# Operand order of small matmuls in three recurrences, and two stretches instead of five for A's score levels

## The chip, the cores and the metric

The kernel runs on one core of one Trainium2 chip. The metric is the device time of one execution in microseconds; a kernel's time is the median over its runs. TensorE (PE) does the matmuls, VectorE (DVE) and ScalarE (ACT) the elementwise work, GpSimd (POOL) small copies and masks, SyncE (SP) issues most DMAs.

## What is computed

One layer with three recurrent mixers over 16 learned tokens and 256 tokens of width 2048: a gated linear recurrence (A), an mLSTM (B) and RWKV-7 (C), each 1024 wide. All start from one projection of the normalised input and end in three gated branch products, one output product and a norm.

```python
xn = rmsnorm(h, norm_g[l])
(a_q, a_f, a_i, a_z, b_q, ..., c_z, g_a, g_b, g_c) = split_cols(xn @ w_in[l])
y_a, y_b, y_c = hgrn2_mixer(...), mlstm_mixer(...), rwkv7_mixer(...)
merged = (sigmoid(g_a) * (y_a @ w_br[l, 0]) + sigmoid(g_b) * (y_b @ w_br[l, 1])
          + sigmoid(g_c) * (y_c @ w_br[l, 2]))
h = h + merged @ w_out[l]
# A, in one chunk: scores with a decay between positions t and s, channel by channel
att = einsum('bhtd,bhsd,bhtsd->bhts', q, k, pair_decay(cg, cg, causal_mask(length)))
# C, in one chunk: a unit lower triangular solve, then outputs and the next state
u = triangular_solve(eye(length) - l_ab, rhs)
y = einsum(r * exp(cw), s_mat) + r_b @ u + r_k @ v
s_mat = exp(cw[-1]) * s_mat + (b * tail).T @ u + (k * tail).T @ v
```

## The kernel before

**Gemms.** Weights stream in as f32 tiles `raw` (SP queue). ACT casts each to `wh`, DVE subtracts to get the remainder `wl`; the activations are split in the same way (`xH`, `xL`). Each product is three fp32r matmuls, and all of them are named `gp<-...` in the trace after their PSUM tile. Blocks run in a fixed list: the projections of the groups of B, C and A, then for each of the branches B, C, A four pairs of a gate product and a branch product, then the output product. These gemms fill TensorE from 16 us to the end.

**Scans.** The recurrences are Python generators that put their small instructions between the gemm matmuls: `b_scan` (4 heads), `c_scan` (4 groups, PSUM tile `cbank`) and `a_scan` (4 groups, PSUM tile `bank`). A planner (`Order`) advances a generator as the gemm's planned clock moves on, and the framework's scheduler then places every instruction of every engine in one static program, by its own estimate of when its operands are written. TensorE runs its program in order. So where a scan's matmuls are not all estimated ready at the same time, the scheduler puts gemm matmuls between them.

**The places that the change touches.** A *stretch* here is a run of scan matmuls with no gemm matmul between them. All matmuls of the scans except those on `bonesR`, `onesR` with split operands, `wups` and `sel`, and the transposes, are plain f32, and the trace has two records for each of them.

- `colsum` sums a split operand over partitions: first with its high half `h` (written by ACT), then with its low half `l` (written later, by DVE).
- `c_scan`, after its solve: products with `VT` and then `ZT` build the inverse's off-diagonal block, over `p` = 0, 1. `VT` comes by two DMAs, `p` = 0 first. Two copies write `ZT`, `X` and `UV` for the two halves `p`: DVE that of `p` = 0, ACT that of `p` = 1 (`ZT`: ACT both). In each of five chunks: `UV,SC`, `cX,Vm`, then the state product `UV,BT` (four matmuls, `p` = 0 then 1, chunks 0 to 3), then the output products `SC,UV` and `RA,Zs`.
- `a_scan` builds the scores of a 32 by 32 block in five levels, pair by pair: level 4 from `Kb`, `Qb`, levels 0 to 3 from tiles `W` of half width 16, 8, 4 and 2. Each level has two DVE subtractions (`aE`), an exponential on ACT, two DVE products (`aW`), and then `small(li, ...)`, 16 or 18 matmuls of 32 columns. The score levels go to two PSUM banks `pss` and are masked and summed after the last level. `aE`, `aW`, `aKb`, `aQb`, `aC`, `aLF` share a pool of six buffers (tag `wx`).

The first product of branch B (tile `yHB`, the cast of B's result) needs room that the pool of C frees only after its fourth scan; on TensorE it follows the first gate block (`gp<-wh,xH 128x512` and its like).

Of the kernel before, what the change touches and what calls it, by code (L numbers as in the profile page):

```python
# [150 lines left out]
def kernel(  # L151
# [33 lines left out]
    def mm(o, lhsT, rhs, start, stop):  # L185
        nc.tensor.matmul(o, lhsT, rhs, start=start, stop=stop)  # L186
        n = 1
        for d in rhs.shape[1:]:
            n *= d
        od.cost("pe", max(n, 256) / 2400 + 0.003 if lhsT.dtype == F32R else max(4 * n / 2400, 0.04 if lhsT.shape[1] <= 32 else 0.1))  # L190
# [23 lines left out]
    def cbank():  # L214
        return cps.tile([P, 512], F32, name="cbank", tag="s")

    def wc(shape, name, dt=F32):
        return ev.tile(shape, dt, name=name, tag="wc", bufs=6)

    def wx(shape, name, dt=F32):  # L220
        return ev.tile(shape, dt, name=name, tag="wx", bufs=6)
# [8 lines left out]
            yield  # L230

    def colsum(o, w, h, l):
        mm(o, w, h, start=True, stop=False)
        mm(o, w, l, start=False, stop=True)

    def low(l, x, h):
        V.tensor_tensor(out=l, in0=x, in1=h.bitcast(F32), op=ALU.subtract)
# [269 lines left out]
    def c_scan(g, st):  # L507
# [32 lines left out]
        for j in range(2):  # L540
            ps = cbank()
            colsum(ps[:, 0:T], bonesR, HL[:, 0, j, :], HL[:, 1, j, :])
            V.tensor_scalar(out=SQ[:, j, :], in0=ps[:, 0:T], scalar1=1e-24, scalar2=None, op0=ALU.max)
# [26 lines left out]
        for cc in (0, 2, 4):  # L570
# [3 lines left out]
            w = P if n == 2 else 2 * NMETA  # L574
# [46 lines left out]
        for j in range(2):  # L621
            colsum(ps[:, j * SEQ:(j + 1) * SEQ], bonesR, RH[:, j, :], RL[:, j, :])
# [73 lines left out]
        ps = cbank()  # L696
        psz = ps.rearrange("s (q k) -> s q k", k=32)
        ZT = wc([P, 8, 32], "ZT")
        for c in range(4):
            for p in range(2):  # L700
                for j in range(2):
                    r = 64 * p + 32
                    q = 64 * (1 - p)
                    mm(psz[r:r + 32, 4 * j + c, :], SC[q:q + 32, j, c, 0, p, 32:64], VT[q:q + 32, 5 * j + c, :],
                       start=True, stop=True)
        for p in range(2):
            r = 64 * p + 32
            S.copy(out=ZT[r:r + 32], in_=psz[r:r + 32, 0:8, :])
        yield "pe"
        ps = cbank()  # L710
        psz = ps.rearrange("s (q k) -> s q k", k=32)
        for c in range(4):
            for p in range(2):
                for j in range(2):
                    r = 64 * p + 32
                    mm(psz[64 * p:64 * p + 32, 4 * j + c, :], ZT[r:r + 32, 4 * j + c, :], Vm[r:r + 32, j, c, p, 32:64],
                       start=True, stop=True)
# [13 lines left out]
        for c in range(5):  # L731
            nq = 64 if c < 4 else NMETA

            ps = cbank()
            psv = ps.rearrange("s (j p v) -> s j p v", j=4, p=2)
            for j in range(2):
                mm(psv[:, j], SC[:, j, c, 0].rearrange("s p t -> s (p t)"), UV[:, c, j].rearrange("s p v -> s (p v)"), start=True, stop=True)
            X = cp.tile([P, 2, 64], F32, name="cX", tag="cX")
            for p in range(2):
                hs = slice(64 * p, 64 * p + 64)  # L740
                (S.copy if p else V.tensor_copy)(out=X[hs], in_=psv[hs, 0:2, p, :])
            yield "pe"
            ps = cbank()
            psv = ps.rearrange("s (j v) -> s j v", v=64)
            for j in range(2):
                mm(psv[:, j, :], Vm[:, j, c].rearrange("s p t -> s (p t)"), X[:, j, :], start=True, stop=True)
            for p in range(2):
                (S.copy if p else V.tensor_copy)(out=UV[64 * (1 - p):64 * (1 - p) + 64, c, :, p, :],
                                                 in_=psv[64 * p:64 * p + 64, 0:2, :])
            yield "pe"  # L750
            if c < 4:
                ps = cbank()
                psv = ps.rearrange("s (j v) -> s j v", v=64)
                for j in range(2):
                    for p in range(2):
                        hs = slice(64 * p, 64 * p + 64)
                        mm(psv[hs, j, :], BT[:, j, c, hs], UV[:, c, j, p, :], start=True, stop=True)
                Sn = cp.tile([P, 2, 64], F32, name="cS", tag="cS", bufs=2)
                el = E1[:, :, 64 * c + 63:64 * c + 64].broadcast_to([P, 2, 64])
                if St is None:  # L760
                    V.tensor_tensor(out=Sn, in0=psv[:, 0:2, :], in1=el, op=ALU.mult)
                else:
                    V.tensor_tensor(out=Sn, in0=psv[:, 0:2, :], in1=St, op=ALU.add)
                    V.tensor_tensor(out=Sn, in0=Sn, in1=el, op=ALU.mult)
                for p in range(2):
                    (S.copy if p else V.tensor_copy)(out=UV[64 - 64 * p:128 - 64 * p, c + 1, :, p, :],
                                                     in_=Sn[64 * p:64 * p + 64])
            after = od.ready
            ps = cbank()
            psv = ps.rearrange("s (j v) -> s j v", v=64)  # L770
            for j in range(2):
                for p in range(2):
                    mm(psv[64 * p:64 * p + 64, j, 0:nq], UV[:, c, j, p, :], SC[:, j, c, 1, p, 0:nq], start=True, stop=St is None)
                if St is not None:
                    for p in range(2):
                        mm(psv[64 * p:64 * p + 64, j, 0:nq], cst["Zs"][:, p, j, :], RA[:, 1, j, 64 * c:64 * c + nq], start=False, stop=True)
            S.copy(out=Yt[:, :, 64 * c:64 * c + nq], in_=psv[:, 0:2, 0:nq])
            if c < 4:

                for p in range(2):  # L780
                    nc.gpsimd.tensor_copy(out=cst["Zs"][64 * p:64 * p + 64, p], in_=Sn[64 * p:64 * p + 64])
                St = Sn
                od.ready = max(after, od.ready - 0.5)
            yield "pe"
# [11 lines left out]
        for j in range(2):  # L796
            colsum(ps[:, j * SEQ:(j + 1) * SEQ], bonesR, SH[:, j, :], SL[:, j, :])
# [340 lines left out]
    def a_scan(g, st):  # L1138
# [20 lines left out]
        def small(li, lk, lq):  # L1159
            for j in range(2):  # L1160
                pv = pss[j][:, 0:320].rearrange("s (b l t) -> s b l t", b=2, l=5)
                for b in range(8):
                    r = 32 * (b % 4)
                    mm(pv[r:r + 32, 1 - b // 4, li, :], lk[:, j, 32 * b:32 * b + 32], lq[:, j, 32 * b:32 * b + 32],
                       start=True, stop=True)
                if li:
                    o = 320 + 16 * (li - 1)
                    mm(pss[j][96:128, o:o + 16], lk[:, j, T - 32:T], lq[:, j, SEQ:T], start=True, stop=True)


        Kb = wx([P, 2, T], "aKb")
        Qb = wx([P, 2, T], "aQb")
# [3 lines left out]
        S.activation(out=f2(Kb)[:, :, 1], in_=f2(LF)[:, :, 1], func=AF.Exp, scale=-1.0)  # L1176
        V.tensor_tensor(out=f2(Qb)[:, :, 1], in0=f2(Q)[:, :, 1], in1=f2(G)[:, :, 1], op=ALU.mult)
        V.tensor_tensor(out=f2(Kb)[:, :, 1], in0=f2(Kb)[:, :, 1], in1=f2(K)[:, :, 1], op=ALU.mult)
        yield "pe"
        small(4, Kb, Qb)  # L1180

        for li, hf in enumerate((16, 8, 4, 2)):
            W = wx([P, 2, T], f"aW{hf}")
            E = wx([P, 2, T], "aE")
            if hf == 16:
                view = lambda a: a[:, :, 0:SEQ].rearrange("p j (b e) -> p j b e", e=32)
                nb = [P, 2, 8, 16]
            else:
                view = lambda a: a.rearrange("p j (b e) -> p (j b) e", e=2 * hf)
                nb = [P, 2 * T // (2 * hf), hf]  # L1190
            Cv, Ev, Wv, Kv, Qv = (view(a) for a in (C, E, W, K, Q))
            ref = Cv[..., hf - 1:hf].broadcast_to(nb)
            od.ready = od.clk["pe"]
            V.tensor_tensor(out=Ev[..., 0:hf], in0=ref, in1=Cv[..., 0:hf], op=ALU.subtract)
            V.tensor_tensor(out=Ev[..., hf:], in0=Cv[..., hf:], in1=ref, op=ALU.subtract)
            full = (lambda a: a[:, :, 0:SEQ]) if hf == 16 else (lambda a: a)
            S.activation(out=full(E), in_=full(E), func=AF.Exp)
            yield
            V.tensor_tensor(out=Wv[..., 0:hf], in0=Ev[..., 0:hf], in1=Kv[..., 0:hf], op=ALU.mult)
            V.tensor_tensor(out=Wv[..., hf:], in0=Ev[..., hf:], in1=Qv[..., hf:], op=ALU.mult)  # L1200
            yield "pe"
            small(li, W, W)
            yield

        M2 = wx([P, 2, 2, 32], "aM2")
# [99 lines left out]
        for j in range(2):  # L1305
            o = po[:, j * SEQ:(j + 1) * SEQ]
# [204 lines left out]
    for u in range(KT // UK):  # L1511
        h, l = ws.next()
        unit(h, l, u, KT, gw[0][:, 0:T], xH, xL, 0, T, slice(0, P))
        h, l = ws.next()
# [100 lines left out]
    for n, (c0, m) in enumerate(outs):  # L1615
        ps = [gps.tile([P, 512], F32, name="gp", tag="g") for _ in range(2)]
        us = KT * m // 1024
        if n < len(outs) - 1:
            for u in range(us):
                h, l = ws.next()  # L1620
# [55 lines left out]
```

## Time and profile before

| | us |
|---|---|
| runs (3), median | 1255.44 (1253.87 to 1256.13) |
| the profiled execution, its own time | 1253.23 |
| its span, first to last instruction | 1251.5 |
| PE busy | 1228.9 (98%) |
| PE weight load busy | 1114.4 (89%) |
| DVE busy | 875.4 (70%) |
| ACT busy | 661.2 (53%) |

The chain that ended last lies 89% on PE, 6% on DVE, 2% on ACT. Records of matmuls overlap, and their ends are modelled, so the busy time of PE says only that it was hardly ever empty; how fast it works is read from the distance between the starts of neighbouring records. 9226 records stand for 8212 matmuls. The mean granted clock is 0.994.

### The profile page before, as it was taken

To read this page: it belongs to the slowest core of one execution; us is meant where nothing else is said; L and a number is where in the kernel's file an instruction comes from. 1 tells how busy PE (TensorE), PEld (TensorE's weight loads), DVE (VectorE), ACT (ScalarE), POOL (GpSimd) and SP (SyncE) were. 2 spreads that over 40 slices of the span, in tenths; PEclk is the share of its full clock that TensorE was granted. 3 is DMA by queue.
4 is the path that set the end of the run, shared out by engine and by line. 5 is a ranking of instruction groups with operands and counts; after the bars stand their busy time and mean duration, and the time that the engine had idled before them with its cause. 6 is when DMAs were issued, how large, how long until landed. Compare 5 with 4: busy or idle time off the path is not lost.

```text
span 1251.5 us, 23069 instructions
## 1 busy us (share of the span) xinstructions
PE 1228.9 (98%) x9226; PEld 1114.4 (89%) x9226; DVE 875.4 (70%) x1485; ACT 661.2 (53%) x1028; POOL 51.3 (4%) x167
## 2 busy tenths in 40 slices
PE   8999999999999999999999999999999999999997
PEld 8999999999998999989999987888888888888887
DVE  6688996698975889976789985644555565555554
ACT  6765445664445764656665655544444444444444
POOL 3100000000050000000000000000000000000000
PEclk8999999999999999999999999999999999999999
DMA  8646564465563554444554453566766666665563
GB/s 227 189 140 172 153 177 127 119 172 160 152 168 87 169 167 137 144 137 122 161 162 138 128 174 107 187 197 187 223 196 187 191 213 201 190 194 171 186 199 120
DMA packets 173125, 207.43 MB, mean 166 GB/s; under 512 B 22396, under 2 KB 127225, under 8 KB 172633
## 3 DMA queue, kind: packets, MB, share of 16 engines
q1 hardware_dynamic: 172104, 202.73, 55.3%
q0 software_dynamic: 880, 3.22, 0.7%
q8 instruction: 72, 1.18, 0.4%
q14 instruction: 37, 0.30, 0.1%
q10 hardware_dynamic: 32, 0.01, 0.0%
HBM read 202.19 MB, written 3.74 MB: 165 GB/s over the span
## 4 chain that ended last, share of the span: by engine, by line
PE 89%; DVE 6%; ACT 2%; issue 1%; DMA 1%; SPq 0%; ACTq 0%; DVEq 0%
PE gp L186 79%; PE cbank L186 5%; PE bank L186 3%; DVE wl L127 2%; ACT wh L127 1%; PE cbank L193 1%; DMA xt<-in_x_dram 1%; PE bank L193 1%; DVE aM L127 0%; DVE LV L127 0%; DVE BK L127 0%; DVE aY L127 0%; DVE Ltmp L127 0%; DVE UV L127 0%; DVE SC L127 0%
## 5 line engine op out<-in xcount | busy, mean ns | idle before, releaser
L127 DVE TENSOR_TENSOR wl<-raw,wh 128x1024 fp32r<-128x1024 f32 (+1 forms) x370 | 449.0, 1215 | 250.1 <-ACT wh L127 247.9
L127 ACT CAST wh<-raw 128x1024 fp32r<-128x1024 f32 (+1 forms) x370 | 386.3, 1045 | 398.3 <-PE gp L186 369.6
L186 PE MATMUL gp<-xH,wh 128*128 128x272 f32 (+3 forms) x1552 | 450.3, 290 | 0.5 <-DVE cK L127 0.3
L186 PE MATMUL gp<-xH,wl 128*128 128x272 f32 (+3 forms) x1552 | 444.8, 287 | 3.6 <-DVE wl L127 3.6
L186 PE MATMUL gp<-xL,wh 128*128 128x272 f32 (+3 forms) x1552 | 445.4, 287 | 0.0
L186 PEld LDWEIGHTS gp<-xH,wl 128*128 128x128 f32 x1552 | 293.0, 189 | 4.9 <-DVE wl L127 4.2
L186 PEld LDWEIGHTS gp<-xH,wh 128*128 128x128 f32 x1552 | 293.3, 189 | 3.2 <-DVE cK L127 0.5
L186 PEld LDWEIGHTS gp<-xL,wh 128*128 128x128 f32 x1552 | 293.1, 189 | 1.1 <-DVE xL L127 0.2
L186 PE MATMUL gp<-wh,xH 128*128 128x512 f32 x384 | 152.6, 397 | 0.0
L186 PE MATMUL gp<-wh,xL 128*128 128x512 f32 x384 | 152.0, 396 | 0.0
L186 PE MATMUL gp<-wl,xH 128*128 128x512 f32 x384 | 150.9, 393 | 0.0
L186 PEld LDWEIGHTS gp<-wh,xL 128*128 128x128 f32 x384 | 72.1, 188 | 17.5
L186 PEld LDWEIGHTS gp<-wl,xH 128*128 128x128 f32 x384 | 72.3, 188 | 16.0
L186 PEld LDWEIGHTS gp<-wh,xH 128*128 128x128 f32 x384 | 72.2, 188 | 15.8
L186 PE MATMUL gp<-wh,mH 128*128 128x512 f32 (+1 forms) x144 | 51.1, 355 | 0.0
L186 PE MATMUL gp<-wl,mH 128*128 128x512 f32 (+1 forms) x144 | 51.0, 354 | 0.0
L186 PE MATMUL gp<-wh,mL 128*128 128x512 f32 (+1 forms) x144 | 50.9, 354 | 0.0
L127 DVE TENSOR_TENSOR Ltmp<-LU,LV 40x31 f32<-40x31 f32 (+15 forms) x124 | 41.0, 331 | 2.5 <-DMA LU<-scr 0.3
L127 DVE TENSOR_TENSOR LV<-LV,Ltmp 40x31 f32<-40x31 f32 (+15 forms) x124 | 41.0, 331 | 2.4
L186 PEld LDWEIGHTS gp<-wh,mL 128*128 128x128 f32 x144 | 27.2, 189 | 3.8
L186 PEld LDWEIGHTS gp<-wh,mH 128*128 128x128 f32 x144 | 27.2, 189 | 3.8
L186 PEld LDWEIGHTS gp<-wl,mH 128*128 128x128 f32 x144 | 27.2, 189 | 3.6
(410 smaller groups left out, 1488.5 us busy)
## 6 DMA issues: line engine op xcount, KB each, us to landing
raw<-in_w_in_dram SPq DMA_DIRECT2D x288, 512.0 KB, 3.6
raw<-in_w_br_dram SPq DMA_DIRECT2D x48, 512.0 KB, 4.2
raw<-in_w_out_dram SPq DMA_DIRECT2D x32, 512.0 KB, 3.5
hres<-in_x_dram POOLq DMA_DIRECT2D x2, 1024.0 KB, 6.6
raw<-in_w_in_dram SPq DMA_DIRECT2D x4, 256.0 KB
fg<-in_final_norm_g_dram POOLq DMA_DIRECT2D x1, 1024.0 KB, 4.5
out_dram<-hres SPq DMA_DIRECT2D x4, 256.0 KB, 2.3
xt<-in_x_dram SPq DMA_DIRECT2D x3, 320.0 KB, 4.9
```

The lines of the kernel that those rows point to most:

```text
L127: r = f(*a, **k)
L186: nc.tensor.matmul(o, lhsT, rhs, start=start, stop=stop)
L193: nc.tensor.transpose(o, a, i)
```

## The change

Three things. `colsum` multiplies the low half first. In `c_scan` five loops over `p` go over 1, 0 instead of 0, 1, so that the first matmul of each group reads the half that is written last. In `a_scan` the first level is not multiplied at once: levels are collected, and after half widths 8 and 2 the collected ones are multiplied, the newest first. The order of additions within the sums is not touched, apart from `colsum`.

```diff
     def colsum(o, w, h, l):
-        mm(o, w, h, start=True, stop=False)
-        mm(o, w, l, start=False, stop=True)
+        mm(o, w, l, start=True, stop=False)
+        mm(o, w, h, start=False, stop=True)
...
         for c in range(4):
-            for p in range(2):
+            for p in (1, 0):
...
                 for j in range(2):
-                    for p in range(2):
+                    for p in (1, 0):
                         hs = slice(64 * p, 64 * p + 64)
                         mm(psv[hs, j, :], BT[:, j, c, hs], UV[:, c, j, p, :], start=True, stop=True)
...
             for j in range(2):
-                for p in range(2):
+                for p in (1, 0):
                     mm(psv[64 * p:64 * p + 64, j, 0:nq], UV[:, c, j, p, :], SC[:, j, c, 1, p, 0:nq], start=True, stop=St is None)
                 if St is not None:
-                    for p in range(2):
+                    for p in (1, 0):
...
-        yield "pe"
-        small(4, Kb, Qb)
+        todo = [(4, Kb, Qb)]
...
-            yield "pe"
-            small(li, W, W)
+            todo.append((li, W, W))
+
+            if hf in (8, 2):
+                yield "pe"
+                while todo:
+                    small(*todo.pop())
             yield
```

Built, both programs have 8212 matmuls. Those of the scans stand in 200 stretches before and in 170 after: `UV,BT` heads 30 and then 16, `SC,UV` 8 and 4, products with `VT` 6 and 3, with `ZT` 6 and 3, `cX,Vm` 19 and 20, stretches with A's levels 17 and 8, transposes 37 and 39; the rest is equal in number.

PE, first group of C, second chunk from the end of its state products (`UV,BT`, the state product; `gp`, a gemm). Before:

```order
L186 MATMUL gp<-xH,wl 128x272
L186 MATMUL cbank<-UV,BT 64x64
L186 MATMUL gp<-xH,wh 128x272
L186 MATMUL cbank<-UV,BT 64x64 x3
L186 MATMUL cbank<-SC,UV 64x64 x2
L186 MATMUL cbank<-RA,Zs 64x64 x2
```

After, the corresponding chunk:

```order
L186 MATMUL gp<-xL,wh 128x272
L186 MATMUL gp<-xH,wl 128x272
L186 MATMUL gp<-xH,wh 128x272
L186 MATMUL cbank<-UV,BT 64x64 x4
L186 MATMUL cbank<-SC,UV 64x64 x2
L186 MATMUL cbank<-RA,Zs 64x64 x2
```

The one matmul that stood alone has joined the other three; this holds at 14 of the 16 state products (two were whole before).

PE, first group of A, the score levels (`aW_5985`: half width 8; `aW_5873`: 16; `aQb,aKb`: level 4; before, 16 is `aW_5978`). Before, the level of half width 16 alone, between gemm matmuls:

```order
L186 MATMUL gp<-xH,wh 128x256
L186 MATMUL gp<-xL,wh 128x256
L186 MATMUL gp<-xH,wl 128x256
L186 MATMUL bank<-aW_5978 32x32 x16
L186 MATMUL gp<-xH,wh 128x256
```

After:

```order
L186 MATMUL gp<-xH,wl 128x256
L186 MATMUL bank<-aW_5985 32x32 x8
L186 MATMUL bank<-aW_5985 32x16
L186 MATMUL bank<-aW_5985 32x32 x8
L186 MATMUL bank<-aW_5985 32x16
L186 MATMUL bank<-aW_5873 32x32 x16
L186 MATMUL bank<-aQb,aKb 32x32 x8
L186 MATMUL bank<-aQb,aKb 32x16
```

Three levels follow each other; the other two (half widths 2 and 4) stand in a second stretch. In the second and the fourth group C's `VT` or `ZT` products stand inside A's second stretch.

ACT, around the first cast of B's result (`yHB`), where the fourth scan of C ends (`cY`: its output copy; `cSq`, `cSH`: squares for its norm; `ATT`: scores of A's fourth group). Before:

```order
L127 COPY cY<-cbank 128x2x16
L127 COPY ATT<-bank 32x2x64
L127 ACTIVATE cSq_9721<-cY 128x512
L127 ACTIVATE cSH<-cY 128x512
L127 COPY ATT<-bank 32x2x32
L127 COPY ATT<-bank 128x144
L127 COPY ATT<-bank 128x16
L127 ACTIVATE sg<-gp 128x512 x2
L127 ACTIVATE cSq_9721<-cbank,epsc 128x512
L127 CAST yHB<-yB 128x512
```

After:

```order
L127 COPY UV<-cbank 64x2x64
L127 COPY cY<-cbank 128x2x16
L127 CAST yHB<-yB 128x512
L127 ACTIVATE cSq_9728<-cY 128x512
L127 ACTIVATE cSH<-cY 128x512
```

The cast has moved ahead of the squares, the score copies and the gate's `sg`. On PE the last output product of C (`SC,UV`, `RA,Zs` of the fifth chunk) stood one gemm matmul ahead of the first product with `yHB`; now 21 gemm matmuls stand between them. C's fourth scan as a whole stands some 20 gemm matmuls earlier: its `VT` products follow gemm matmul 4742 before and 4722 after.

## Rows read from the trace of the kernel before

**Rows 1.** The page, busy time of each engine, its share and its instructions.

```profile
PE 1228.9 (98%) x9226; PEld 1114.4 (89%) x9226; DVE 875.4 (70%) x1485; ACT 661.2 (53%) x1028; POOL 51.3 (4%) x167
```

**Rows 2.** Waits of PE: who waited for whom, us in total, times, longest.

```profile
PE gp L186 <- DVE wl L127: 3.6, 3, 1.5
PE gp L186 <- ACT yHB L127: 1.3, 1, 1.3
```

**Rows 3.** Timeline of PE, a split state product: start, us, engine, what, records.

```profile
216.10 0.29 PE L186 MATMUL gp<-xL,wh 128*128 128x272 f32 x1
216.23 0.29 PE L186 MATMUL gp<-xH,wl 128*128 128x272 f32 x1
216.45 0.33 PE L186 MATMUL cbank<-UV,BT 128*64 128x64 f32 x2
216.71 0.39 PE L186 MATMUL gp<-xH,wh 128*128 128x272 f32 x1
217.03 0.39 PE L186 MATMUL cbank<-UV,BT 128*64 128x64 f32 x5
...
218.10 0.29 PE L186 MATMUL gp<-xH,wl 128*128 128x272 f32 x1
```

**Rows 4.** Timeline of PE, a state product in one piece, last group.

```profile
755.47 0.39 PE L186 MATMUL gp<-wh,xH 128*128 128x512 f32 x1
755.70 0.40 PE L186 MATMUL gp<-wl,xH 128*128 128x512 f32 x1
756.03 0.49 PE L186 MATMUL cbank<-UV,BT 128*64 128x64 f32 x8
...
757.25 0.40 PE L186 MATMUL gp<-wh,xH 128*128 128x512 f32 x1
```

**Rows 5.** Timeline of PE, two stretches of A: 36 and 108 records.

```profile
469.23 0.29 PE L186 MATMUL gp<-xH,wl 128*128 128x272 f32 x1
469.44 0.57 PE L186 MATMUL bank<-aQb,aKb 128*32 128x32 f32 x36
...
470.18 0.30 PE L186 MATMUL gp<-xL,wh 128*128 128x272 f32 x1
...
484.47 0.28 PE L186 MATMUL gp<-xH,wl 128*128 128x256 f32 x1
484.68 1.33 PE L186 MATMUL bank<-aW 128*32 128x32 f32 x108
...
486.17 0.29 PE L186 MATMUL gp<-xL,wh 128*128 128x272 f32 x1
```

**Rows 6.** Timeline of PE, where C's fourth scan ends.

```profile
767.70 0.50 PE L186 MATMUL gp<-wh,xL 128*128 128x512 f32 x1
...
769.48 0.38 PE L186 MATMUL cbank<-cSH,bonesR 128*128 128x256 f32 x1 [0.85 <-ACT cSH L127]
...
772.15 0.80 PE L186 MATMUL gp<-wh,yHB 128*128 128x512 f32 x1 [1.28 <-ACT yHB L127]
772.74 0.63 PE L186 MATMUL gp<-wl,yHB 128*128 128x512 f32 x1
773.17 0.63 PE L186 MATMUL gp<-wh,yHB 128*128 128x512 f32 x1
```

**Rows 7.** Windows: us, busy PE, PEld, DVE, ACT, POOL, PE clock, DMA.

```profile
450.00:530.00 80.00, 78.17 (x811) 76.12 (x810) 74.83 (x170) 47.56 (x80) 0.32 (x2) 1.00 0.51 144
640.00:730.00 90.00, 86.52 (x962) 83.46 (x961) 81.78 (x185) 50.85 (x84) 0.13 (x1) 1.00 0.53 149
772.00:775.00 3.00, 2.85 (x7) 2.27 (x8) 2.43 (x4) 3.00 (x7) 0.00 (x0) 0.50 0.02 5
```

**Rows 8.** Timeline of DVE and ACT, the two copies ahead of that state product.

```profile
755.38 0.28 DVE L127 COPY UV<-cbank 64x128 f32<-64x128 f32 x1 [1.10 <-PE cbank L186]
...
755.76 0.26 ACT L127 COPY UV<-cbank 64x128 f32<-64x128 f32 x1
```

**Rows 9.** Waits of DVE for PE, the one at A's levels.

```profile
DVE aW L127 <- PE bank L186: 1.8, 1, 1.8
```

More of the change, by code (lines that the diff above doesn't have):

```diff
@@ L771, in c_scan @@
             for j in range(2):
-                for p in range(2):
+                for p in (1, 0):
                     mm(psv[64 * p:64 * p + 64, j, 0:nq], UV[:, c, j, p, :], SC[:, j, c, 1, p, 0:nq], start=True, stop=St is None)
                 if St is not None:
-                    for p in range(2):
+                    for p in (1, 0):
                         mm(psv[64 * p:64 * p + 64, j, 0:nq], cst["Zs"][:, p, j, :], RA[:, 1, j, 64 * c:64 * c + nq], start=False, stop=True)
```

## Prediction

> **What bounds the kernel now.** I read the page's busy times first, then who waited for whom on TensorE, then TensorE's timeline at the places that the change touches, then windows. TensorE is busy for 98% of the span [rows 1], and what it waits for is small: the two longest kinds are 3.6 us for the split weights `wl` and 1.3 us for `yHB` [rows 2]. So it is bound by what TensorE itself does, and a microsecond taken off its program counts in full while DVE and ACT keep up with the weights. Busy says nothing about speed, though. In a run of gemm matmuls the starts lie 0.13 us apart (272 columns, 216.10 to 216.23 [rows 3]) or 0.23 us (512 columns, 755.47 to 755.70 [rows 4]). Wherever a stretch of the scans' small f32 matmuls is put in, the starts around it are much further apart than the small matmuls account for. That loss at the seams is what the change can take away, and it never shows as a wait.
>
> **What a stretch costs beside its matmuls.** Two stretches of A differ in length alone. From the start of the last gemm matmul before to that of the second one after it take 470.18 - 469.23 = 0.95 us with 36 records and 486.17 - 484.47 = 1.70 us with 108 [rows 5]. Less two gemm matmuls at 0.12 to 0.13, that is 0.69 and 1.45 us. A record costs (1.45 - 0.69) / 72 = 0.011 us, so 36 of them 0.38, and the stretch as such 0.69 - 0.38 = 0.31 us.
>
> The state product of C gives the price of a split directly. Split, with one gemm matmul between, it takes 218.10 - 216.23 = 1.87 us, three gemm matmuls included [rows 3]: 1.87 - 3 x 0.13 = 1.48. In one piece it takes 757.25 - 755.70 = 1.55 us with two [rows 4]: 1.55 - 2 x 0.23 = 1.09. The split costs 0.39 us.
>
> **The change part by part.**
>
> - State products: 14 pieces fewer, at 0.39: 5.5 us.
> - A's levels: 17 stretches become 8, 9 x 0.31 = 2.8 us. The matmuls are the same ones.
> - The other small pieces that join (`SC,UV` 4, `VT` 3, `ZT` 3): nearest are the two prices above, so between 3.1 and 3.9; in the middle, 10 x 0.35 = 3.5 us.
> - One more stretch of `cX,Vm` and two more of transposes: at most 3 x 0.31 = 0.9 lost, at least nothing, since transposes are another kind; I take 0.5.
> - `colsum`: its four matmuls are of the gemms' kind, with no seam to save. Nothing, as long as the low half, now read first, is there; where the second matmul waited for it, the first will.
>
> Together 5.5 + 2.8 + 3.5 - 0.5 = 11.3 us, all on TensorE.
>
> Then the end of C's fourth scan. There TensorE has run out of gemm matmuls: the next need `yHB`, and C must finish first. Between 767.70 and 772.15 it waits 0.85 us for `cSH` and 1.28 us for `yHB` [rows 6]. After that its clock is at half: 0.50 in the window from 772 to 775, that is 1.2 instead of 2.4 GHz [rows 7], and the starts lie 0.43 us apart (772.74 to 773.17 [rows 6]). The seven gemm matmuls that begin there take 775 - 772.15 = 2.85 us, where 7 x 0.23 = 1.6 would do: 1.2 us lost. In the changed program C's last products stand 21 gemm matmuls ahead of the first that needs `yHB`, instead of one, and the cast stands ahead of the squares. 21 x 0.23 = 4.8 us cover what took 4.45 us from 767.70 on. So waits and clock loss go: 0.85 + 1.28 + 1.2 = 3.3 us, with bounds of 0 (C isn't really earlier) and 4.3 (4.45 less one gemm matmul, some 1.1 us of transposes and norm sums, plus the clock).
>
> What is late next is `wl`. Six of the nine stretches of A that go (first, third and fourth group) lie in or at the edge of the windows where DVE is nearly full: 74.83 of 80 us and 81.78 of 90 [rows 7]. The order of every engine is new there, and the stalls of 3.6 us [rows 2] will fall differently, between all gone and twice as long. With a slightly faster TensorE I add 1.3 us.
>
> The sum is 11.3 + 3.3 - 1.3 = 13.3 us: the profiled execution's 1253.2 would become 1239.9. The median of the runs is 2.2 us above that execution, so I forecast 1255.4 - 13.3 = **1242 us**.
>
> **A's pool of six buffers.** Until the first of its two stretches is done, `aC`, `aKb`, `aQb`, both `aW` and the `aE` in work hold all six buffers, so DVE's product for half width 4 waits for TensorE, and queued `wl` wait behind it. Before, DVE waited so once, for 1.8 us [rows 9]. A split of a 256 wide block feeds 24 matmuls, 24 x 0.12 = 2.9 us, and three are in hand. A wait under 8.6 us therefore starves nobody; I count nothing.
>
> **Rivals.**
>
> *The wait takes the seam's place.* TensorE now stands at the first matmul until the later copy is done, with all gemm matmuls behind it. DVE's copy ends at 755.66 and ACT's at 756.02, 0.36 us later [rows 8]; if the stretch stands where its first piece stood, 18 stretches (14 state and 4 output products) wait so long: 6.5 us back, 1249. For it: the scheduler places by estimates. Against it: in the rows of the program the whole stretch stands where its second piece stood, in most chunks six or more gemm matmuls behind `cX,Vm`, and today the second piece begins without one (217.03 [rows 3]). The Trainium skill bears on this (TensorE: Matmul & The Clock Gate, section on packing small matmuls, "The mechanism"): matmuls run in strict order of the program, none overtakes another. By that rule a late operand at the head blocks the gemm behind it, and the sum would be this rival's; the trace, which has the old order, shows no such wait ahead of the second piece, and cannot show the new heads.
>
> *DVE is the bound in A's part.* Then the six stretches' 6 x 0.31 = 1.9 us don't come and the stalls for `wl` double; less the 1.3 us already added that is 1.9 + 3.6 - 1.3 = 4.2 us worse than the forecast, 1246. For it: 91 to 94% in the two windows [rows 7]. Against it: three stalls in all [rows 2].
>
> *C's end is no earlier.* The 3.3 us stay: 1245. For it: the shift by 20 gemm matmuls is the scheduler's estimate. Against it: DVE's solve of that group, which leads to it, moved ahead in DVE's own queue as well.
>
> *The cost belongs to the matmuls, not to the seams.* Then joining saves nothing and 1255.4 - 3.3 + 1.3 leaves 1253, no change that can be told. Against it: the two stretches of A differ threefold in records and only by 0.011 us a record [rows 5].
>
> *Slower.* The wait for buffers, above: DVE far ahead of TensorE stands at the product for half width 4 while its `wl` queue behind it. It decides from about 8.6 us a time. With 13 us in each of four groups it costs 4 x 4.4 = 17.6 us, and the time is 1260. For it speaks only the one wait of 1.8 us [rows 9].
>
> **How the numbers follow.** Forecast 0.56 (1237 to 1245), wait at the head 0.13, DVE bound 0.11, C's end no earlier 0.11, no gain at the seams 0.06, slower 0.03. A measurement of this kernel can tell about 0.2%, 2.5 us, from no change. Of the wait and the DVE rival I give 0.03 to their coming together, within 2.5 us of before: faster 0.88, same 0.09, slower 0.03. The low end, 1237, is the sum with each of the 33 stretches that join at 0.39 (12.9 less 0.5), 4.3 at C's end and 1.7 us less waiting for `wl`: 18.4 us less. The high end, 1249, takes in the first three rivals.
>
> **What would show it.** Right: state products all as x8 in the timeline, a seam count lower by 30, no wait for `cSH` or `yHB` near 760 and no half clock there, waits of TensorE for `wl` under 5 us. Wrong: waits of TensorE for `UV` or `SC` of several microseconds; `wl` above 7 us; a wait of DVE for TensorE at `aW` of more than 8 us; or joined stretches that take as long as their pieces.

## The result, and the profile after

| | before | after |
|---|---|---|
| median of the runs, us | 1255.24 (1253.87 to 1256.13) | 1239.15 (1237.35 to 1240.90) |
| the profiled execution, its own time, us | 1253.23 | 1237.61 |
| its span, us | 1251.5 | 1235.9 |

The ratio is 0.9872, with an interval from 0.9857 to 0.9886: 16.1 us less, where 13.3 were forecast. 1239.15 lies inside the range, 2.9 us below the forecast.

The page's busy line of after answers to [rows 1]:

```profile
PE 1213.2 (98%) x9226; PEld 1105.9 (89%) x9226; DVE 876.2 (71%) x1485; ACT 661.4 (54%) x1028; POOL 56.5 (5%) x167
```

The same 9226 records keep TensorE busy for 15.7 us less, while DVE and ACT do what they did before. Nothing was taken out of the program, so what went is the time around the records.

TensorE's waits, the answer to [rows 2] (who waited for whom, us in total, times, longest):

```profile
...
PE gp L186 <- DVE wl L127: 1.6, 4, 0.7
PE bank L186 <- DVE aW L127: 1.6, 2, 0.9
...
PE bank L186 <- DVE aYL L127: 1.2, 2, 0.8
PE cbank L186 <- ACT cX L127: 0.9, 3, 0.3
PE cbank L186 <- issue: 0.6, 1, 0.6
...
PE cbank L186 <- ACT UV L127: 0.4, 1, 0.4
```

`yHB` and `cSH` are gone from the list, and `wl` fell from 3.6 to 1.6 us, where the forecast had let it grow. New are two waits for `aW`, and three short ones for `cX` (ACT's copy of `X`). The wait for ACT's copy of `UV`, with which a state product now begins, shows once, with 0.4 us.

Where the time went is read from the starts of the gemm matmuls, since both programs have the same 6896 of them in the same order, but for 18 in two places (12 around number 4600, 6 around 4790). The table gives the time between the starts of gemm matmuls of the same number (us), for the two kernels and for the two experiments that make one part of the change alone:

| from gemm matmul | to | what lies there | before | C's part alone | A's part alone | after |
|---|---|---|---|---|---|---|
| 650 | 2630 | C, groups 1 and 2; B | 307.73 | 301.82 | 307.75 | 301.84 |
| 2630 | 4530 | C, group 3; A, groups 1 to 3 | 291.98 | 290.50 | 291.07 | 288.63 |
| 4530 | 4870 | C and A, group 4, C's end | 91.06 | 90.66 | 85.21 | 84.09 |
| 4870 | 6895 | rest | 447.58 | 447.60 | 447.53 | 447.56 |

After saves 5.9, 3.3 and 7.0 us in the first three rows and nothing in the last: 16.2 us. Between the start and gemm matmul 650 these four differ by up to 1.3 us with the loads at the beginning, and nothing is read from that.

**A state product in one piece.** TensorE's timeline of after, first group of C, the second chunk from the end of its state products, as in [rows 3] (start, us, engine, what, records):

```profile
213.35 0.29 PE L186 MATMUL gp<-xH,wh 128*128 128x272 f32 x1
213.56 0.45 PE L186 MATMUL cbank<-UV,BT 128*64 128x64 f32 x8
...
214.41 0.39 PE L186 MATMUL gp<-xL,wh 128*128 128x272 f32 x1
214.64 0.28 PE L186 MATMUL gp<-xH,wl 128*128 128x272 f32 x1
```

From 213.35 to 214.64 are 1.29 us; less two gemm matmuls at 0.13 that is 1.03. In two pieces it took 1.48 [rows 3]. The join saved 0.45 us here.

**C's end.** The answer to [rows 6], and the window that answers to the half clock of [rows 7] (us, busy PE, PEld, DVE, ACT, POOL, PE clock, DMA share, GB/s):

```profile
757.16 0.39 PE L186 MATMUL gp<-wh,xL 128*128 128x512 f32 x1
757.39 0.82 PE L193 MATMUL bank<-ident,aV 128*128 128x128 f32 x6
757.96 0.48 PE L186 MATMUL gp<-wh,yHB 128*128 128x512 f32 x1
758.27 0.40 PE L186 MATMUL gp<-wl,yHB 128*128 128x512 f32 x1
```

```profile
750.00:790.00 40.00, 40.00 (x209) 33.41 (x209) 28.20 (x35) 26.32 (x46) 0.57 (x1) 1.00 0.57 179
```

The first product with `yHB` follows without a wait, the next start is 0.31 us behind it instead of 0.59, and the clock stays at its full level (1.00, 2.4 GHz) where it had been at half.

**The new waits.** A's second stretch in its first group, on TensorE:

```profile
480.14 0.29 PE L186 MATMUL gp<-xH,wh 128*128 128x272 f32 x1
481.37 0.95 PE L186 MATMUL bank<-aW 128*32 128x32 f32 x72 [0.94 <-DVE aW L127]
482.25 0.39 PE L186 MATMUL gp<-xL,wh 128*128 128x272 f32 x1
...
661.83 0.95 PE L186 MATMUL bank<-aW 128*32 128x32 f32 x72 [0.65 <-DVE aW L127]
```

The stretch heads with the level that DVE writes last, and TensorE stands there, 0.94 us in the first and 0.65 in the third group, with the gemm matmul behind it ready (that one has no wait of its own).

### The profile page after: what moved, and what is told of

It is laid out like the page before. It is cut to its first block, busy times and chain, and to the rows that moved or that the text cites. A ratio compares the mean times of both kernels' runs of the same rounds, so it can differ in the third digit from the quotient of the medians.

```text
span 1235.9 us, 23061 instructions
## 1 busy us (share of the span) xinstructions
PE 1213.2 (98%) x9226; PEld 1105.9 (89%) x9226; DVE 876.2 (71%) x1485; ACT 661.4 (54%) x1028; POOL 56.5 (5%) x167
## 4 chain that ended last, share of the span: by engine, by line
PE 83%; DVE 10%; ACT 3%; issue 2%; DMA 1%; SPq 0%; ACTq 0%; DVEq 0%
PE gp L186 75%; PE cbank L186 4%; DVE wl L127 3%; PE bank L186 3%; ACT wh L127 1%; DVE Ltmp L127 1%; DVE LV L127 1%; PE cbank L193 1%; PE bank L193 1%; DMA xt<-in_x_dram 1%; DVE UV L127 0%; DVE aM L127 0%; DVE aY L127 0%; ACT L127 0%; DVE aW L127 0%
## 5 line engine op out<-in xcount | busy, mean ns | idle before, releaser
L186 PEld LDWEIGHTS gp<-wl,xH 128*128 128x128 f32 x384 | 72.3, 188 | 16.1
L186 PEld LDWEIGHTS gp<-wh,xH 128*128 128x128 f32 x384 | 72.1, 188 | 15.7
```

## Experiments

Four kernels isolate or alter parts of the change; seven measure the price of a stretch by itself, with extra matmuls.

**`colsum` alone.**

```diff
-        mm(o, w, h, start=True, stop=False)
-        mm(o, w, l, start=False, stop=True)
+        mm(o, w, l, start=True, stop=False)
+        mm(o, w, h, start=False, stop=True)
```

> Only the sum over partitions multiplies its low half first; all else as before. The seam theory (a stretch of plain f32 matmuls between gemm matmuls costs 0.3 to 0.4 us beside its matmuls) expects nothing: the four stretches that join are of the gemms' own kind, so 1255 +-1.5 us, with the wait near 770 for yHB as before. The wait theory (the first matmul now waits for the low half, with the gemm behind it) expects up to 2 us slower, 1257. If the sum's order alone had brought the gain, it would be near 1239.

1254.19 us; ratio 0.9991 (0.9982 to 1.0000). Four stretches fewer, of full-width fp32r matmuls, and no difference that counts: joining them saved nothing that can be told, and reading the low half first cost nothing. C's end did not stay as before, though. The first product with `yHB`, and the window behind it:

```profile
773.21 0.50 PE L186 MATMUL gp<-wh,yHB 128*128 128x512 f32 x1 [0.55 <-ACT yHB L127]
```

```profile
773.00:776.00 3.00, 2.79 (x12) 2.34 (x13) 1.97 (x3) 3.00 (x7) 0.00 (x0) 1.00 0.00 0
```

TensorE waits 1.45 us for `ATT` and 0.55 for `yHB` there, in all nearly as long as before (0.85, 0.21 and 1.28), and yet the clock stays at its full level. From gemm matmul 4530 to 4870 this kernel takes 89.09 us, where before takes 91.06. So the half clock doesn't follow every stall of this length.

**C's five loops alone** (`for p in (1, 0)`, the diff above).

> Only the five loops of the C scan over p go 1, 0; the sum over partitions and A's levels as before. 200 stretches become 175. In the program C's fourth scan ends where it ended before, one gemm matmul ahead of the first product with yHB. Seam theory: 14 x 0.39 + 10 x 0.35 + 0.3 = 9.3 us less, 1246, and the stall near 770 (2.1 us of waits, half clock after) is still there. Wait theory (the head of each stretch waits for the later copy, 0.36 us each in 18): 2.8 us less, 1252, with waits for UV at the heads of the state products.

1246.73 us; ratio 0.9926 (0.9913 to 0.9940). Four of its waits of TensorE, and the window behind the one for `yHB`:

```profile
PE gp L186 <- DVE wl L127: 3.6, 3, 1.5
...
PE cbank L186 <- ACT cX L127: 1.9, 4, 0.7
...
PE gp L186 <- ACT yHB L127: 1.3, 1, 1.3
...
PE cbank L186 <- ACT cSH L127: 0.9, 1, 0.9
```

```profile
764.00:767.00 3.00, 2.76 (x7) 2.19 (x8) 2.35 (x4) 3.00 (x7) 0.00 (x0) 0.50 0.00 0
```

The stall at C's end and the half clock behind it are all still there, and `wl` waits as before. So the 8 us that this part saves come from its stretches that are gone: 25 in all, 24 of them of matmuls that use 32 or 64 of the array's 128 columns, called narrow from here on. In the first row of the table there are 14 narrow ones fewer, and 5.91 / 14 = 0.42 us went with each, though TensorE's waits there grew by 1.0 us (two for `cX`, one for `cK`). In the second and third row 10 went, and only 1.9 us with them, where two more waits for `cX` stand (0.55 and 0.73 us). So new waits took some of the gain back, but far from all that the wait theory had (1252). Which of the five loops brings how much is not parted.

**A's two stretches alone.**

```diff
-        yield "pe"
-        small(4, Kb, Qb)
+        todo = [(4, Kb, Qb)]
...
+            if hf in (8, 2):
+                yield "pe"
+                while todo:
+                    small(*todo.pop())
```

> Only A's five levels are multiplied in two stretches; the loops of C and the sum over partitions as before. 200 stretches become 195, A's own 17 become 8. In the program C's fourth scan ends 24 gemm matmuls ahead of yHB. Theory of two parts: seams 9 x 0.31 = 2.8 us less one VT, two transposes, and the stall at C's end gone, 3.3 us: 5 to 6 us less, 1249 to 1250, no half clock near 765. If the stall's end in the changed kernel came from the C loops instead, only the seams are left: 1252 to 1253. If A's deferred levels make TensorE wait at the second stretch's head (0.7 to 1.0 us in three groups of the changed kernel), 2 to 3 us less gain than the sum.

1248.37 us; ratio 0.9944 (0.9931 to 0.9958). A bit more than expected, and in another place: groups 1 to 3 of A give only 0.9 us (291.98 to 291.07 in the table), the last group with C's end 5.85. Two waits of TensorE, and the window that begins with its first product with `yHB` (768.22):

```profile
PE gp L186 <- DVE wl L127: 2.0, 4, 0.9
PE bank L186 <- DVE aW L127: 1.6, 2, 1.0
```

```profile
768.00:771.00 3.00, 3.00 (x19) 2.66 (x18) 2.93 (x5) 3.00 (x8) 0.00 (x0) 1.00 0.42 108
```

The change of A alone takes the stall at C's end away, so it isn't C's new order that makes C's fourth scan earlier. Why fewer stretches of A have this effect on the scheduler was not looked into. It is A's part as well that brings the waits for `wl` down from 3.6 to 2.0 us, and that brings the waits for `aW`.

**The oldest level first.**

```diff
-                    small(*todo.pop())
+                    small(*todo.pop(0))
```

> The changed kernel, but the collected levels of A are multiplied oldest first instead of newest first. The program has 171 stretches instead of 170. Seam theory: only the count matters, so 0.3 us more than the changed kernel, 1239 to 1241. If beginning with the operand written last is what matters in A too, more splits or waits at A's places and 2 us or more above it.

1238.76 us; ratio 0.9866 (0.9853 to 0.9880): the same as after. Three rows of TensorE's timeline:

```profile
482.23 0.57 PE L186 MATMUL bank<-aW 128*32 128x32 f32 x36 [0.47 <-DVE aW L127]
...
662.73 0.57 PE L186 MATMUL bank<-aW 128*32 128x32 f32 x36 [0.79 <-DVE aW L127]
670.80 0.39 PE L186 MATMUL gp<-xH,wl 128*128 128x272 f32 x1 [1.00 <-DVE wl L127]
```

For A it doesn't matter which level heads the stretch: all but one of its stretches stay whole in either order, and the wait for `aW` moves (0.94 to 0.47 in one group, 0.65 to 0.79 in the other) without going away.

**The price of a stretch, 32 columns.** Extra f32 matmuls that nothing reads, all with data that has long been there, go into the gate products of branches C and A of the changed kernel: 512 of them in 128 stretches of 4 (the diff) or, at every fourth place, in 32 stretches of 16.

```diff
+    def dummy(n):
+        z = cbank()
+        for q in range(n):
+            r = 32 * (q % 4)
+            mm(z[r:r + 32, 0:32], ident[:, 0:32], ident[:, 32:64], start=True, stop=True)
...
                 rows_unit(ps[i], i, u, aH, aL, t0, h, l, kts)
+                if seams["on"] and kts == KT and (2 * u + i) % 1 == 0:
+                    dummy(4)
```

> The changed kernel with 512 added f32 matmuls of 32 x 32 columns (both operands slices of the identity, results unused), in the gate products of branches C and A where no scan runs: 128 stretches of 4, six gemm matmuls of 512 columns apart. Price of a seam 0.31 us, of a record 0.011 us: 128 x 0.31 + 1024 x 0.011 = 40 + 11 = 51 us above the changed kernel, 1290. If the cost belongs to the matmuls, the same as its twin with 32 stretches of 16.

> The same 512 added matmuls in 32 stretches of 16. 32 x 0.31 + 11 = 21 us above the changed kernel, 1260, so 96 seams x 0.31 = 30 us less than its twin. If the cost belongs to the matmuls: no difference.

1289.79 and 1257.18 us: (1289.79 - 1257.18) / 96 = 0.34 us for a stretch. The rows say the same, of the first kernel and then of the second:

```profile
872.44 0.40 PE L186 MATMUL gp<-wh,xL 128*128 128x512 f32 x1
872.76 0.27 PE L186 MATMUL cbank<-ident 128*32 128x32 f32 x8
872.96 0.50 PE L186 MATMUL gp<-wh,xH 128*128 128x512 f32 x1
873.30 0.39 PE L186 MATMUL gp<-wl,xH 128*128 128x512 f32 x1
```

```profile
876.45 0.40 PE L186 MATMUL gp<-wh,xL 128*128 128x512 f32 x1
876.78 0.46 PE L186 MATMUL cbank<-ident 128*32 128x32 f32 x32
877.16 0.50 PE L186 MATMUL gp<-wh,xH 128*128 128x512 f32 x1
877.50 0.40 PE L186 MATMUL gp<-wl,xH 128*128 128x512 f32 x1
```

Less two gemm matmuls at 0.23, the short stretch takes 873.30 - 872.44 - 0.46 = 0.40 us and the long one 1.05 - 0.46 = 0.59. 24 records more cost 0.19, or 0.008 each; eight records are 0.06, and 0.34 belong to the stretch. The loss sits at three starts (the middle one read from the single records): the first small one stands 0.32 behind the gemm's, where gemm starts are 0.23 apart, the gemm 0.13 behind the last small one (a record further on in the stretch 0.01), and the next gemm 0.34 behind that.

**64 columns.** The same with `ident[:, 0:64]` as weights, in two column groups by turns.

> The changed kernel with 512 added f32 matmuls of 64 columns of weights (two column groups by turns, 32 moving columns) in its gate products, in 128 stretches of 4. If the price of a stretch belongs to all matmuls that use part of the columns, as the 0.39 us of C's state product (64 columns) beside the 0.31 us of A (32 columns) say, each stretch costs 0.3 to 0.4 us beside its 8 records of some 0.02 us: 128 x 0.5 = 64 us above the changed kernel, 1290 to 1310 us. If it belongs to 32 columns alone and 64 behave as full width, 0.09 us a stretch and up to 0.11 a record: about 1350 us, no lower.

> The same 512 matmuls of 64 columns in 32 stretches of 16. Against the twin with 128 stretches: 96 x 0.35 = 34 us less (29 to 38) if a stretch of 64 columns has the price of the scans' stretches; 9 us less if it has the price of a full-width one. The clock should stay, since 32 records of 0.02 us make less than 1 us.

1310.64 and 1278.86 us: 31.8 / 96 = 0.33 us. The price is the same with 64 columns. The Trainium skill (TensorEngine Tiling (Array Packing), "Key Properties") says that a change of the tiling mode drains TensorE, without a price. The runs are in keeping with it and give 0.33 to 0.34 us for the way there and back; that the time goes to a drain, no run shows by itself.

**Full width.** The same with all 128 columns (`mm(z[:, 0:32], ident, ident[:, 32:64])`).

> As the first, but each added matmul has a weight of the full 128 columns (f32, 32 columns moving), so that only the number type differs from the gemm, not the part of the array. If the seam comes of going to a part of the array and back, its price falls to below 0.1 us and the kernel is within 10 us of its twin with 32 stretches; if it comes of plain f32 beside split operands, 96 x 0.31 = 30 us above that twin.

> The twin of the third, 32 stretches of 16: the seams' share is 32 instead of 128 of them; the matmuls' own share (each record some 0.06 to 0.11 us, as weights of 128 columns must be loaded: 60 to 110 us in all) is the same in both.

1353.55 and 1392.30 us: the joined twin is 38.8 us slower, which no theory had. The mean granted clock of its profiled execution is 0.965, of the other 0.994. One of its stretches, and the windows around it:

```profile
887.91 3.92 PE L186 MATMUL cbank<-ident 128*128 128x32 f32 x32
891.64 0.77 PE L186 MATMUL gp<-wh,xH 128*128 128x512 f32 x1
892.21 0.63 PE L186 MATMUL gp<-wl,xH 128*128 128x512 f32 x1
...
894.35 0.50 PE L186 MATMUL gp<-wh,xH 128*128 128x512 f32 x1
```

```profile
889.00:891.00 2.00, 2.00 (x20) 2.00 (x19) 1.23 (x1) 0.16 (x1) 0.00 (x0) 1.00 0.69 244
891.00:893.00 2.00, 2.00 (x9) 1.78 (x9) 0.00 (x0) 0.00 (x0) 0.00 (x0) 0.54 0.61 169
```

TensorE is busy throughout, yet behind a stretch of 3.7 us with 32 moving columns the clock falls to half (0.54 in that window), and the gemm matmuls start 0.43 instead of 0.23 us apart for some 3 us. That is so behind 21 of the 32 stretches. A mean clock lower by 0.029 over 1390 us is 40 us, which accounts for the 38.8. To part the clock from the seam, a third twin has stretches half as long.

> The changed kernel with 512 full-width f32 matmuls (128 columns of weights, 32 moving columns) added to its gate products, in 64 stretches of 8 instead of 128 of 4 or 32 of 16. In the rows of the 128 and the 32 stretches a record of this kind takes 0.11 us, and a stretch as such 0.09 us (0.003 late at its first record, 0.09 at the gemm matmul behind it), and behind most of the 32 long stretches (3.5 us each) the granted clock is at half for about 3 us. If the long twin was slower by its clock alone, this one, with stretches of 1.8 us, keeps the clock: 1353.6 - 64 x 0.09 = 1348 us. If the clock falls behind stretches of this length as well, it lies above 1355 us. If a full-width stretch costs as much as a 32-column one, 0.34 us, it is 1332 us.

1352.86 us, with a mean clock of 0.996. So the clock was the cause, and the forecast of 1348 was still wrong, since 64 stretches fewer saved 0.7 us, 0.01 each. The rows of the 128 stretches and of the 64:

```profile
874.21 0.39 PE L186 MATMUL gp<-wh,xL 128*128 128x512 f32 x1
874.44 0.97 PE L186 MATMUL cbank<-ident 128*128 128x32 f32 x8
...
875.57 0.39 PE L186 MATMUL gp<-wl,xH 128*128 128x512 f32 x1
```

```profile
873.86 0.39 PE L186 MATMUL gp<-wh,xL 128*128 128x512 f32 x1
874.09 1.86 PE L186 MATMUL cbank<-ident 128*128 128x32 f32 x16
...
876.11 0.39 PE L186 MATMUL gp<-wl,xH 128*128 128x512 f32 x1
```

1.36 - 0.46 = 0.90 us for 8 records and 2.25 - 0.46 = 1.79 for 16: twice as long, so all of it goes with the records, 0.11 us each, and nothing with the stretch. These are f32 like the small ones, so the price of a seam is not one of f32 beside fp32r.

## Why the prediction was right, point by point

**The bound.** Right. TensorE is 98% busy before and after, the span falls with its busy time, while DVE and ACT do unchanged work; what TensorE waits for is a few us before and after.

**The price of a seam.** Right, and measured by itself: 0.33 to 0.34 us, where two stretches of A [rows 5] had given 0.31 and the split state product [rows 3, 4] 0.39. In the kernel it is rather more: 5.89 us for the 14 narrow stretches that after has less in the table's first row, 0.42 each. Over the whole 33 narrow ones went, which is 11.2 us at 0.34 and 13.9 at 0.42, where the sum had 11.3 after 0.5 for new stretches. That term was needless: full-width stretches cost 0.01.

**A's levels.** 9 x 0.31 = 2.8 us were counted, and the seams are gone, but A's part alone saves just 0.9 in the first three groups, where six of the nine would have given 1.9. The step that failed is that a joined stretch was priced by its seam alone. Its head needs a level that DVE has only just written, and the two waits for `aW` took 1.6 us back (and with A's part alone a stretch of `VT` is added, while the waits for `wl` in these groups fell by 1.2, so the account is rough). It is the rival of the wait in the seam's place, at a place where it hadn't been looked for. The rule of the Trainium skill named beside that rival (TensorE: Matmul & The Clock Gate, "The mechanism", on the strict order of matmuls) holds there: the gemm matmul at 482.25 stood behind a head that wasn't ready.

**That rival at its own place.** 18 stretches were to wait 0.36 us for ACT's later copy. Of the 16 state products one shows such a wait, 0.43 us at 727.80. The rows of DVE and ACT ahead of the joined state product at 213.56 (its rows on TensorE stand further up), which answer to [rows 8]:

```profile
212.87 0.28 DVE L127 COPY UV<-cbank 64x128 f32<-64x128 f32 x1 [0.70 <-PE cbank L186]
...
213.24 0.26 ACT L127 COPY UV<-cbank 64x128 f32<-64x128 f32 x1 [1.12 <-DVE UV L127]
```

ACT's copy still ends 0.35 us behind DVE's (213.50 to 213.15), and the stretch begins at 213.56, 0.21 behind the gemm matmul ahead of it, as the first piece did before (216.23 to 216.45). So the scheduler put the whole behind the later copy, as the prediction read from the program, and gemm matmuls cover it. The cover is thin: six of the sixteen begin 0.05 to 0.06 us after ACT's copy ends. The one at 727.80 is among them, and another, at 545.18, begins some 0.1 us later behind its gemm matmul than is usual.

**C's end.** Right in mechanism, but too small: 3.3 us were counted. From gemm matmul 4783, the last ahead of those with `yHB`, to 4830 before takes 786.42 - 767.70 = 18.72 us and after 770.83 - 757.16 = 13.67, so 5.05 less. C's four norm sums, 0.47 us (753.90 to 754.37), stand ahead of this stretch of time in after, so 4.6 are left for C's end, just above the upper bound of 4.3. The waits and the clock loss are 3.3 of it; of the rest the trace lists only 0.2 us as a wait (for `ATT`), and it went too. That the stall vanishes with A's change alone and stays with C's change alone, the prediction didn't say; it took the change as a whole.

**The waits for `wl`.** This is the term with the wrong sign: 1.3 us were added, and 2.0 went. The two longest of the four that are left, on TensorE (the others are 0.24 and 0.20 us):

```profile
523.81 0.39 PE L186 MATMUL gp<-xH,wl 128*128 128x256 f32 x1 [0.45 <-DVE wl L127]
...
704.95 0.38 PE L186 MATMUL gp<-xH,wl 128*128 128x256 f32 x1 [0.74 <-DVE wl L127]
```

Before there was one of 1.3 us at 678, in A's third group, which has no successor. Why it went isn't settled: it stays with C's part alone (3.6 in total), it is gone with A's part alone and with the whole change, and it is back with 1.0 us at 670.80 when the oldest level heads the stretch. So it seems to hang on how A's matmuls and DVE's products for them lie to each other; no run parts the two, and the cause stays open.

**The sum, then.** The table saves 16.2 us. C's end gave 4.6 and `wl` 2.0; the waits for `aW` took 1.6, and TensorE's other waits behind gemm matmul 650 (`cX`, `aYL` and single ones) grew from 3.5 to 5.1 us and took as much. What is left for the seams is 16.2 - 4.6 - 2.0 + 1.6 + 1.6 = 12.8, or 0.39 for each of 33; it is a remainder, so it agrees with the price of a seam without proving it. Against 13.3 the seams were 1.5 too small, C's end 1.3 and `wl` 3.3, and 3.2 us of new waits were missing. That the forecast came within 2.9 us is in part luck: the 3.3 us of `wl` and the 3.2 of new waits nearly cancel.

**The buffers of A.** Right to count nothing. DVE's waits for TensorE at `aW`, the answer to [rows 9], in rows of DVE's timeline of after:

```profile
534.30 0.44 DVE L127 TENSOR_TENSOR aW<-aE,aK 128x272 f32<-128x272 f32 x1 [0.48 <-PE bank L186]
...
715.62 0.44 DVE L127 TENSOR_TENSOR aW<-aE,aK 128x272 f32<-128x272 f32 x1 [0.79 <-PE bank L186]
```

That is 1.3 us in all, less than the 1.8 before and far from the 8.6 from which `wl` would have come late.

**The other rivals.** DVE as the bound in A's part: the waits for `aW` are of this kind, 1.6 us of the 4.2 it was priced at, and `wl` went the other way. C's end no earlier, and no gain at the seams: both contradicted above.

## What to carry over

A stretch of matmuls that use part of the array's columns costs some 0.34 us between full-width ones here, with 8 records as with 32, and no view shows it as a wait: look at the distance between starts, and bring such matmuls together. Put first the operand that is written last, so that the scheduler has no cause to place gemm matmuls into the rest (in C it joined the pieces; for A's levels the order didn't matter); then look whether the head of the joined stretch has cover, since a late one holds up everything behind it. Joining can also lose: the 512 full-width matmuls with 32 moving columns took 38.8 us more in 32 stretches than in 128, because the granted clock fell to half behind 21 of the 32.

## What the runs showed that was not expected

- The clock fell to half with TensorE busy all the time, behind 21 of 32 stretches of 32 full-width records with 32 moving columns (3.5 us). With stretches of 16 such records (1.7 us) the mean clock stayed at 0.996, and with 32 narrow ones (0.4 us with 32 columns, 1.1 us with 64) as well.
- With 32 moving columns a full-width f32 record takes 0.11 us, one of 64 columns 0.029 (the two twins differ by 96 stretches alone, so it is read from two rows: 1.25 us for 32 records less 0.56 for 8, over 24), and one of 32 columns 0.008. A matmul that uses a part of the columns is far cheaper than one that uses all, until the 0.34 us of its stretch are added.
